# A unit of products with its low-weight matmuls set between the high-weight ones

## The chip, the core and the metric

The kernel runs on one core of one Trainium2 chip. The metric is the device time of one execution, in microseconds; "the time before" is the median of three runs of the kernel before.

## The reference

One layer of a streaming encoder for 512 frames of width 2048. The rows of `x` are normalised and multiplied by one wide matrix `w_in` (2048 x 12292): queries, keys, values and gates of three token mixers with four heads each, four forget-gate logits, and three merge gates of width 2048. The mixers are three kinds of attention (softmax with a forget bias, softmax over chunks with a relative bias, stick-breaking). Their outputs are gated, multiplied by `w_up`, weighted by the merge gates, summed, multiplied by `w_out` and added to `x`. All inputs and outputs are float32.

```python
hn = rmsnorm(x, norm_g)
proj = jnp.einsum('bsd,dc->bsc', hn, w_in)
br = proj[..., :QKVG_COLS].reshape(b, s, N_BRANCH, 4, BRANCH_W)
gates = jax.nn.sigmoid(proj[..., QKVG_COLS + N_HEADS:] + b_gate)
...                                    # ya, yb, yc: the three mixers
ys = jnp.stack([from_heads(ya), from_heads(yb), from_heads(yc)], axis=2)
ys = ys * jax.nn.silu(br[:, :, :, 3])
up = jnp.einsum('bsnw,nwd->bsnd', ys, w_up)
merged = jnp.sum(gates * up, axis=2)
return x + jnp.einsum('bsd,de->bse', merged, w_out)
```

## The kernel before

**Precision.** Every float32 operand is split into a high part (a rounded copy, written by ScalarE in `split`, L243) and a low part (the rest, by VectorE, L247). A product is the sum of three: high by high, high weights by low data, low weights by high data. In the names of the profile, `wh` and `wl` are the high and low weights; `x`, `t`, `m` and `y` are data that lie in `Parts`: 256 columns high, and beside them the same 256 columns low.

**Pairs, tasks and units.** The products with `w_in` and `w_out` are grouped by two blocks of 128 output columns (`PairTask`). A task replaces the eight products of a 2 x 2 block scheme (two column blocks, two halves of the frames, two halves of the inner width) by seven products of sums and differences, in the manner of Strassen. Each of the seven is a `Unit`: weights of eight tiles of 128 x 128, `UK = 8`, against eight data tiles of 256 frames. In a unit, the high weights of tile `j` meet high and low data in one matmul of 512 columns, which writes both halves of a PSUM bank; the low weights meet the high data in one of 256 columns, which adds to the left half. When the unit is done, ScalarE or VectorE takes the bank out (`after_of`), adding the two halves. A unit called `single` (the first task of the kernel, the first task with `w_out`, the last unit of all) uses only 256-column matmuls: two with high weights for each tile, one with low. The products with `w_up` (`up_units`) are plain ones with 512 columns throughout.

**The order.** The order of instructions on TensorE, ScalarE and VectorE is written out by a planner (`Flow`): each task is a generator that yields the engine, the cost and sometimes the due time of its next step, or an event that it waits for, and the planner picks the step that can start first. `mm_us` is the cost it takes for a matmul. The stream of units (`stream`, L1610) runs one unit after the other, with a slack so large that attention steps go first where they are ready; the weights are split two units ahead (`LA = 2`, three buffers for each of `wh` and `wl`). On TensorE the order is kept as planned: a matmul that waits holds up what stands behind it.

Within a unit (`mms_of`, L650) the order is: wait for `u.ready_hi` (ScalarE's split done; in `stream`), the eight products with high weights, wait for `u.ready` (VectorE's split done), the eight with low weights. All matmuls of this kind are issued by the helper `mm`, so they show as L262 in the profile.

Of the kernel before, what the change touches and what calls it, by code (L numbers as in the profile page):

```python
# [25 lines left out]
UK = 8  # L26
NQ = 4
HS = S // 2
# [7 lines left out]
PE, ACT, DVE = 0, 1, 2  # L36
# [112 lines left out]
def mm_us(n, x=1):  # L149
    return x * max(0.115, n / 2400 + 0.0133)  # L150
# [11 lines left out]
def hybrid_kernel(  # L162
# [16 lines left out]
    wp = ctx.enter_context(tc.tile_pool(name="wp", bufs=3))  # L179
    tp = ctx.enter_context(tc.tile_pool(name="tp", bufs=NT))  # L180
    sp = ctx.enter_context(tc.tile_pool(name="sp", bufs=8))
# [11 lines left out]
    spawn, set_, give = flow.spawn, flow.set, flow.give  # L193
    t2s, atts, raws, xps = Slots(NT, KEPT), Slots(4), Slots(NR), Slots(NX)
    accs = [Slots(2), Slots(1), Slots(1)]
# [7 lines left out]
    def acc(i=0):  # L203

        return pa.tile([P, S], F32, tag=f"acc{i}", name=nm("acc"), bufs=1 if i else 2)
# [10 lines left out]
    LH, RH = slice(0, HS), slice(HS, S)  # L216

    def two(ap):

        return ap.rearrange("p (h s) -> p h s", h=2)  # L220
# [40 lines left out]
    def mm(ps, w, x, start=False, stop=False, more=False):  # L261
        nc.tensor.matmul(ps, w, x, start=start, stop=stop, skip_group_check=more)  # L262
# [329 lines left out]
    class PairTask:  # L592
# [57 lines left out]
        def mms_of(self, i):  # L650
            p = self.order[i]
            bank = (0, 1, 2, 0, 0, 1, 2)[i] if self.late else {2: 1, 5: 2, 3: 2}.get(p, 0)
            onto = None if self.late else {6: 1, 7: 6, 4: 7, 3: 5}.get(p)
            more = onto is not None
            single = self.late or self.plain_end and p == 4
            self.bank = getattr(self, "bank", {})
            self.bank[p] = bank

            def go(u):
                if more:  # L660
                    yield self.ev[onto]
                    self.ps[p] = self.ps[onto]
                else:
                    yield accs[bank], 1
                    self.ps[p] = acc(bank)

                for j in range(UK):
                    yield lambda: self.ops[p](j) is not None
                    r, _, ev = self.ops[p](j)
                    yield ev  # L670
                    if single:
                        yield PE, mm_us(HS)
                        mm(self.ps[p][:, LH], u.hi[:, j, :], r[:, 0, :], j == 0 and not more, more=more)
                    else:
                        yield PE, mm_us(S)
                        mm(two(self.ps[p]), u.hi[:, j, :], r, j == 0 and not more, more=more)
                    if single:
                        yield PE, mm_us(HS)
                        mm(self.ps[p][:, LH], u.hi[:, j, :], r[:, 1, :], more=more)
                yield u.ready  # L680
                for j in range(UK):
                    yield PE, mm_us(HS)
                    mm(self.ps[p][:, LH], u.lo[:, j, :], self.ops[p](j)[1], stop=j == UK - 1, more=more)
            return go

        def after_of(self, i):
# [946 lines left out]


NT = 21
KEPT = 1
NX = 28
NR = 6
# [47 lines left out]
```

## Time and profile before

| | before |
|---|---|
| time, median of 3 runs | 1340.83 us (1339.83 to 1341.17) |
| span of the profiled execution, the only time that the profile gives for it | 1338.6 us |
| TensorE busy, matmuls | 1326.8 us (99%), 7546 |
| TensorE weight loads | 1158.2 us (87%), 7546 |
| VectorE busy | 1141.3 us (85%) |
| ScalarE busy | 806.2 us (60%) |
| granted TensorE clock | 1.000 |

The profile is of one execution. `PE` is TensorE's matmuls, `PEld` its weight loads, `DVE` VectorE, `ACT` ScalarE, `POOL` GpSimd, `SP` SyncE. A row of the timeline has start, length, engine, line, operation, output and inputs, the partitions and columns, and the count of like neighbours merged into it; a row of a group has a count, the busy time, the mean length of one in ns, and the idle time before it with what ended it. Matmuls are pipelined and their recorded ends are modelled, so neighbours overlap in the record: the pace is read from the starts.

### The profile page before, as it was taken

How to read it: one execution, taken by the hardware profiler on the slowest of the kernel's cores; microseconds unless marked ns; L12 is line 12 of the kernel's file. 1: busy time of each engine (PE TensorE's matmuls, PEld its weight loads, DVE VectorE, ACT ScalarE, POOL GpSimd, SP SyncE). 2: the span in 40 equal slices, each digit the busy share in tenths (PEclk: the TensorE clock that was granted, in tenths of full speed). 3: DMA queues.
4: the chain of work that ended last, by engine and by line, in shares of the span. 5: the costliest groups of instructions: out<-in, count | busy, mean ns of one | idle time of the engine just before them, and what ended most of it. 6: DMA issues, size and time to landing. Idle time of an engine off the chain costs nothing.

```text
span 1338.6 us, 20292 instructions
## 1 busy us (share of the span) xinstructions
PE 1326.8 (99%) x7546; PEld 1158.2 (87%) x7546; DVE 1141.3 (85%) x1691; ACT 806.2 (60%) x1274; POOL 97.9 (7%) x129
## 2 busy tenths in 40 slices
PE   8999999999999999999999999999999999999998
PEld 5888888888888888888888888888888888898887
DVE  7899888878888898888988879888888877797786
ACT  7766656556566655666567665566566645464443
POOL 0000000010100000000110100000010000000100
PEclk9999999999999999999999999999999999999999
DMA  9876677777776777777777677677777755659883
GB/s 307 231 194 163 174 190 201 184 187 181 185 218 163 209 200 182 210 175 197 201 189 190 171 203 189 183 186 189 187 182 250 281 197 177 202 152 258 239 243 103
DMA packets 92707, 265.23 MB, mean 198 GB/s; under 512 B 10528, under 2 KB 17312, under 8 KB 92608
## 3 DMA queue, kind: packets, MB, share of 16 engines
q1 hardware_dynamic: 72928, 202.77, 45.6%
q0 software_dynamic: 15552, 56.63, 25.6%
q10 hardware_dynamic: 4128, 4.53, 1.0%
q8 instruction: 59, 0.97, 0.3%
q14 instruction: 40, 0.33, 0.1%
HBM read 244.19 MB, written 19.70 MB: 197 GB/s over the span
## 4 chain that ended last, share of the span: by engine, by line
PE 96%; DVE 2%; DMA 1%; issue 0%; ACT 0%; DVEq 0%
PE acc L262 82%; PE att L262 8%; DMA raw<-in_w_col 1%; PE att L1124 1%; DVE wl L247 1%; PE att L1052 1%; PE att L257 1%; PE att L1200 1%; PE att L258 1%; PE att L1201 1%; PE att L259 1%; PE att L1199 1%; PE att L1151 0%; DVE m L247 0%; PE att L1302 0%
## 5 line engine op out<-in xcount | busy, mean ns | idle before, releaser
L247 DVE TENSOR_TENSOR wl<-raw,wh 128x1024 fp32r<-128x1024 f32 (+2 forms) x419 | 500.1, 1197 | 145.5 <-ACT wh L243 138.8
L243 ACT ACTIVATE wh<-raw 128x1024 fp32r<-128x1024 f32 (+2 forms) x419 | 434.6, 1039 | 135.6 <-PE acc L262 65.7
L262 PE MATMUL acc<-x,wh 128*128 128x512 f32 (+1 forms) x1568 | 400.5, 391 | 7.0 <-ACT wh L243 7.0
L262 PEld LDWEIGHTS acc<-x,wh 128*128 128x128 f32 x1568 | 277.3, 189 | 56.3 <-ACT wh L243 7.7
L262 PE MATMUL acc<-t,wh 128*128 128x512 f32 (+1 forms) x1128 | 282.2, 389 | 0.0
L262 PEld LDWEIGHTS acc<-t,wh 128*128 128x128 f32 x1128 | 198.5, 189 | 33.5
L262 PEld LDWEIGHTS acc<-x,wl 128*128 128x128 f32 x1504 | 207.0, 190 | 18.0 <-issue 1.7
L262 PE MATMUL acc<-x,wl 128*128 128x256 f32 (+1 forms) x1504 | 216.8, 285 | 0.6 <-DVE wl L247 0.6
L262 PEld LDWEIGHTS acc<-t,wl 128*128 128x128 f32 x1104 | 151.8, 190 | 11.4
L262 PE MATMUL acc<-t,wl 128*128 128x256 f32 x1104 | 156.2, 283 | 0.0
L282 POOL DMA_DIRECT2D raw<-in_w_col x92 | 79.7, 866 | 932.4 <-DMA raw<-in_w_col 469.0
L262 PE MATMUL acc<-m,wh 128*128 128x512 f32 (+1 forms) x512 | 114.1, 366 | 0.3 <-DVE m L247 0.2
L262 PEld LDWEIGHTS acc<-m,wh 128*128 128x128 f32 x512 | 85.4, 189 | 13.7 <-DVE m L247 1.1
L765 ACT ACTIVATE u<-acc 128x512 f32<-128x512 f32 x52 | 31.1, 599 | 75.3 <-PE acc L262 71.8
L819 ACT ACTIVATE c<-acc 128x256 f32<-128x256 f32 x51 | 19.6, 384 | 93.7 <-PE acc L262 90.6
L786 ACT ACTIVATE u<-acc 128x512 f32<-128x512 f32 x51 | 30.3, 594 | 72.7 <-PE acc L262 72.7
L635 DVE TENSOR_TENSOR raw<-raw,raw 128x1024 f32<-128x1024 f32 x54 | 65.8, 1219 | 0.4
L641 DVE TENSOR_TENSOR raw<-raw,raw 128x1024 f32<-128x1024 f32 x54 | 65.8, 1218 | 0.3
L262 PE MATMUL att<-y,wh 128*128 128x512 f32 x256 | 65.8, 389 | 0.0
L262 PEld LDWEIGHTS acc<-m,wl 128*128 128x128 f32 x448 | 60.5, 190 | 4.5 <-DVE wl L247 0.9
L262 PE MATMUL acc<-m,wl 128*128 128x256 f32 x448 | 62.6, 283 | 0.4 <-DVE wl L247 0.4
L769 ACT ACTIVATE v<-acc 128x512 f32<-128x512 f32 x52 | 31.2, 600 | 43.8 <-PE acc L262 43.3
(221 smaller groups left out, 1451.8 us busy)
## 6 DMA issues: line engine op xcount, KB each, us to landing
raw<-in_w_col SPq DMA_DIRECT2D x237, 512.0 KB, 4.5
raw<-in_w_col POOLq DMA_DIRECT2D x92, 512.0 KB, 6.8
raw<-in_w_out SPq DMA_DIRECT2D x40, 512.0 KB, 5.4
gl<-c SPq DMA_DIRECT2D x48, 256.0 KB, 4.1
raw<-in_w_up SPq DMA_DIRECT2D x32, 384.0 KB, 3.3
sg<-gl SPq DMA_DIRECT2D x48, 256.0 KB, 5.0
raw<-in_w_out POOLq DMA_DIRECT2D x16, 512.0 KB, 7.1
x<-in_xT SPq DMA_DIRECT2D x16, 256.0 KB, 7.3
```

Source lines behind the costliest of these rows:

```text
L243: nc.scalar.activation(hi, src, AF.Copy)
L247: nc.vector.tensor_sub(lo, src, f(hi))
L257: nc.tensor.matmul(ps, lh, rh, start=start, stop=False, skip_group_check=more)
L258: nc.tensor.matmul(ps, lh, rl, start=False, stop=False, skip_group_check=more)
L262: nc.tensor.matmul(ps, w, x, start=start, stop=stop, skip_group_check=more)
L282: nc.gpsimd.dma_start(to, src, accum_op=ALU.add)
L635: nc.vector.tensor_add(w[1], w[1], w[5])
L641: nc.vector.tensor_add(w[2], w[2], w[1])
L765: nc.scalar.activation(self.u, ps, AF.Copy)
L769: nc.scalar.activation(self.v, ps, AF.Copy)
L786: nc.scalar.activation(self.s, ps, AF.Copy)
L819: nc.scalar.activation(c, ps[:, RH], AF.Copy, scale=-1.0)
```

## The change

In a unit that isn't `single`, the 256-column matmul with the low weights of tile `j - 4` is put ahead of the 512-column matmul of tile `j`, for `j` from 4 to 7; the other four follow behind as before. Writing H for the 512-column matmuls and L for the 256-column ones, `HHHHHHHH LLLLLLLL` becomes `HHHH LHLHLHLH LLLL`. The wait for `u.ready` stands ahead of each L. The planner then writes out the whole order anew.

```diff
@@ mms_of
                     yield accs[bank], 1
                     self.ps[p] = acc(bank)
 
+                def low(j):
+                    yield u.ready
+                    yield PE, mm_us(HS)
+                    mm(self.ps[p][:, LH], u.lo[:, j, :], self.ops[p](j)[1], stop=j == UK - 1, more=more)
+
                 for j in range(UK):
+                    if j >= AHEAD and not single:
+                        yield from low(j - AHEAD)
                     yield lambda: self.ops[p](j) is not None
                     r, _, ev = self.ops[p](j)
                     yield ev
...
                     if single:
                         yield PE, mm_us(HS)
                         mm(self.ps[p][:, LH], u.hi[:, j, :], r[:, 1, :], more=more)
-                yield u.ready
-                for j in range(UK):
-                    yield PE, mm_us(HS)
-                    mm(self.ps[p][:, LH], u.lo[:, j, :], self.ops[p](j)[1], stop=j == UK - 1, more=more)
+                for j in range(0 if single else UK - AHEAD, UK):
+                    yield from low(j)
             return go
...
 NT = 21
+AHEAD = 4
 KEPT = 1
```

## The prediction

> **What bounds the kernel now.** I read the page first, then what TensorE waits for, then its order in time, then groups of matmuls in narrow stretches. Page: the span, TensorE's line, and the chain that ended last.
>
> ```profile
> span 1338.6 us, 20292 instructions
> PE 1326.8 (99%) x7546; PEld 1158.2 (87%) x7546; DVE 1141.3 (85%) x1691; ACT 806.2 (60%) x1274; POOL 97.9 (7%) x129
> PE 96%; DVE 2%; DMA 1%; issue 0%; ACT 0%; DVEq 0%
> ```
>
> TensorE is busy for 99% of the span and carries 96% of the chain. Its two largest waits (us in total, times, longest):
>
> ```profile
> PE acc L262 <- ACT wh L243: 7.0, 3, 6.6
> PE acc L262 <- DVE wl L247: 1.1, 2, 0.6
> ```
>
> They come to 8.1 us, 6.6 of it one wait. So the time changes only if the step from one matmul to the next changes, or if a new wait appears. The edit leaves the set of matmuls as it is; the question is what a step costs in another order. Timeline of TensorE (start, length, count): 256-column matmuls alone (61.70 to 63.62), 512-column ones alone (24 from 1118.52 to 1123.96), and two starts of the units that the edit changes, 43 units apart.
>
> ```profile
> 61.70 2.08 PE L262 MATMUL acc<-x,wh 128*128 128x256 f32 x16
> 63.62 1.12 PE L262 MATMUL acc<-x,wl 128*128 128x256 f32 x8
> ...
> 1118.52 1.98 PE L262 MATMUL acc<-y,wh 128*128 128x512 f32 x8
> ...
> 1123.96 0.39 PE L262 MATMUL att<-y,wh 128*128 128x512 f32 x1
> ...
> 1209.27 2.00 PE L262 MATMUL acc<-m,wh 128*128 128x512 f32 x8
> ...
> 1329.38 2.00 PE L262 MATMUL acc<-m,wh 128*128 128x512 f32 x8
> ```
>
> Alone, a 256 steps (63.62 - 61.70)/16 = 0.120 us and a 512 steps (1123.96 - 1118.52)/24 = 0.2267. A unit of eight and eight should take 8 x 0.2267 + 8 x 0.120 = 2.773 us; it takes (1329.38 - 1209.27)/43 = 2.793. **Each unit loses 20 ns**, with no wait in it. Groups in narrow stretches (count | busy, mean ns of one) show where: the 512s and the 256s of the unit that starts at 299.87, and 512s alone after 1118.
>
> ```profile
> L262 PE MATMUL acc<-x,wh 128*128 128x512 f32 x8 | 2.0, 392 | 0.0
> L262 PE MATMUL acc<-x,wl 128*128 128x256 f32 x8 | 1.1, 282 | 0.0
> L262 PE MATMUL att<-y,wh 128*128 128x512 f32 x9 | 2.5, 389 | 0.0
> ```
>
> Ends of matmuls are modelled: a record is some 162 ns longer than the step (389 against 227), so differences of records are differences of steps. The 512s behind a run of 256s lose 3 ns each, 24 a unit; nothing of the kind shows where sizes stay the same. The loss comes with the change of size.
>
> **The change part by part.** How many units: the low matmuls by form, over the whole span, are
>
> ```profile
> L262 PE MATMUL acc<-x,wl 128*128 128x256 f32 x1472 | 206.3, 282 | 0.6 <-DVE wl L247 0.6
> L262 PE MATMUL acc<-t,wl 128*128 128x256 f32 x1104 | 156.2, 283 | 0.0
> L262 PE MATMUL acc<-m,wl 128*128 128x256 f32 x448 | 62.6, 283 | 0.4 <-DVE wl L247 0.4
> ```
>
> 3024 in all, 378 units of eight, at 283 ns where settled. Two tasks of seven units and the last unit are "single" and stay as they are: 363 units change. In each, 8 high, 8 low becomes 4 high, then a low and a high by turns four times, then 4 low: five rises from 256 to 512 where there was one. The instruction order of the changed kernel shows this throughout; GpSimd and SyncE keep theirs entirely, VectorE and ScalarE but for a few neighbours near the end. No DMA moves, no instruction comes or goes. One nanosecond a unit is 0.363 us.
>
> *Price of a rise with short runs.* No stretch has single 256s between 512s; the nearest have two 512s (L948, L949) between low matmuls, and three 256s of attention (L257 to L259) between high ones:
>
> ```profile
> 204.31 0.86 PE L262 MATMUL acc<-t,wh 128*128 128x512 f32 x3
> ...
> 207.47 0.40 PE L262 MATMUL acc<-x,wh 128*128 128x512 f32 x1
> ...
> 371.41 0.87 PE L262 MATMUL acc<-t,wl 128*128 128x256 f32 x6
> ...
> 372.82 1.33 PE L262 MATMUL acc<-x,wh 128*128 128x512 f32 x5
> ...
> 376.10 0.63 PE L262 MATMUL acc<-t,wh 128*128 128x512 f32 x2
> ```
>
> From 204.31 to 207.47 stand eight 512s and eleven 256s: 3.16 us against 3.134 by the steps alone, 26 ns lost over two rises, 13 each. From 371.41 to 376.10 stand twelve 512s (ten from 372.82 on) and sixteen 256s: 4.69 against 4.640, 50 over two rises, 25 each. So a short run doesn't pass free; but a rise is paid over several 512s, not by the first alone. What one unsettled matmul costs (groups from 372.2 to 375.1, and from 375.4 on):
>
> ```profile
> L262 PE MATMUL acc<-x,wh 128*128 128x512 f32 x8 | 2.2, 396 | 0.0
> L262 PE MATMUL acc<-x,wl 128*128 128x256 f32 x8 | 1.1, 280 | 0.0
> ```
>
> An unsettled 512 loses 7 ns (396 against 389), an unsettled 256 gains 1 to 3 (282 or 280 against 283). In the changed unit no run is long enough to settle, so I take 7 for all eight 512s and -2 for all eight 256s: 56 - 16 = 40 ns a unit where 20 are lost now, **+20 ns, 363 times: +7.3 us**. Bounds: below, the loss vanishes (-20 ns, -7.3 us); above, each of the four added rises costs the full 20 of today's (+80 ns, +29 us). I take the value between because the 396 and 280 rows are the only ones whose surroundings stay unsettled for a whole unit.
>
> [...]
>
> *The low weights are wanted earlier*, by four 512s, 0.91 us, and a low matmul that waits now holds up the high ones queued behind it on TensorE. Three units: an ordinary one, and the two with the least room that I found (TensorE, then VectorE's split that it needs):
>
> ```profile
> 305.45 0.86 PE L262 MATMUL acc<-t,wh 128*128 128x512 f32 x3
> ...
> 685.49 1.12 PE L262 MATMUL acc<-x,wl 128*128 128x256 f32 x8
> ...
> 1205.43 1.21 PE L262 MATMUL acc<-m,wl 128*128 128x256 f32 x8 [0.45 <-DVE wl L247]
> ```
>
> ```profile
> 304.06 1.22 DVE L247 TENSOR_TENSOR wl<-raw,wh 128x1024 fp32r<-128x1024 f32 x1
> 683.35 1.22 DVE L247 TENSOR_TENSOR wl<-raw,wh 128x1024 fp32r<-128x1024 f32 x1
> 1204.16 2.35 DVE L247 TENSOR_TENSOR wl<-raw,wh 128x1024 fp32r<-128x1024 f32 x2
> ```
>
> At 1205.43 the split ends last already; four high matmuls that ran ahead of it now stand behind it: **+0.9 us**. At 685.49 the split ended at 684.57, 0.92 before: just in time. In the ordinary unit it ended at 305.28, and the lows, 0.91 after 305.45, come 1.1 later: free. The last high matmul also ends four lows, 0.48 us, later in its unit, and ScalarE's split for three units on waits for that buffer; the 1.1 cover it. Without that cover each late unit would pay up to 0.9. PSUM is read at the unit's end, which doesn't move.
>
> **Sum.** 7.3 + 0.9 = 8.2 us on the profiled execution, whose span of 1338.6 is 2.2 below the median of the runs, 1340.8; those 2.2 have no part in the change: 1340.8 + 8.2 = **1349.0**.
>
> **The rivals.**
> (a) *No change.* The loss belongs to a unit and not to a rise: 20 ns remain and only the wait is added, 1341.7. For: from 204.31 on two rises cost little more than one. Against: from 371.41 on they cost 50. [...] Chance 0.16.
> (b) *Faster: the run of lows is the cause.* A 256 leaves its successor's load only 120 ns; alone between 512s, each low has a long neighbour that makes up for it, and the 512s behind are at 389 again. Then the 20 ns go: -7.3 + 0.9, 1334.4. It decides if a single low is too short a run to unsettle what follows. Against: the 512s from 372.82 on are at 396 behind a run of only two. Chance 0.22; a further 0.04 that lows also step below 0.120, under 1333.
> (c) *The full price of a rise.* Each added rise costs 20 ns although one 512 follows: +29 + 0.9, 1371. Against: today 24 ns are spread over eight 512s. Chance 0.11.
> (d) *Waits.* The later splits of ScalarE push those of VectorE behind the lows; it decides where a lead falls under 0.91 us. Ten such units cost 9 us on top of (a): 1351. Against: the ordinary lead. Chance 0.03.
>
> **How the numbers follow.** The forecast has 0.44; its own range is 3 to 17 us more (a 512 at 5 to 9 ns, a 256 at -3 to -1), 1344 to 1358. About 0.2% is what a measurement of this kernel can tell from no change: 1338.1 to 1343.5. Faster: (b) with its tail, 0.26. Same: (a), 0.16. Slower: the forecast, (c) and (d), 0.58. The range takes in (b) and the forecast and leaves out (c) and the tail of (b), 0.15: 1333 to 1360.
>
> **What would show it.** Right: TensorE's timeline with units near 2.81 us; groups of 512s in them near 396 and of 256s near 281; a wait near 1205 on VectorE's split, 0.9 longer than now. Wrong: 512s at 389 in the changed units (b), 392 (a), above 400 (c), or waits on the split in many units (d).

## The result, and the profile after

The changed kernel takes 1346.6 us (median of four runs, 1345.2 to 1346.9) where the kernel before takes 1341.0 (1339.8 to 1341.2) beside it: 1.0043 times as long, 95% interval 1.003 to 1.0055. It is slower by 5.6 us. The prediction was 1349.0, range 1333 to 1360.

The page of the changed kernel, the lines that answer to those of before (span; busy time by engine; shares of the chain that ended last):

```profile
span 1345.0 us, 20293 instructions
PE 1331.6 (99%) x7546; PEld 1157.3 (86%) x7546; DVE 1142.9 (85%) x1691; ACT 807.0 (60%) x1274; POOL 97.6 (7%) x129
PE 93%; DVE 3%; DMA 2%; ACT 1%; issue 0%; DVEq 0%; ACTq 0%
```

The span is 6.4 us longer, TensorE is busy 4.8 longer with the same 7546 matmuls, and the other engines' busy times moved by under 2 us. So most of the time went into the pace of matmuls, and some into waits. TensorE's waits (us in total, times, longest):

```profile
PE acc L262 <- ACT wh L243: 7.7, 3, 6.6
PE acc L262 <- DVE wl L247: 2.0, 2, 1.4
```

They are 9.7 us where they were 8.1: 0.9 more on VectorE's split of low weights, 0.7 more on ScalarE's of high ones. The second lies near 59 us, in the kernel's first task, whose units are `single`; the first unit that the edit changes starts at 81 us. TensorE's timeline there, before and after:

```profile
58.72 2.18 PE L262 MATMUL acc<-x,wh 128*128 128x256 f32 x16 [0.23 <-ACT wh L243]
...
59.28 2.17 PE L262 MATMUL acc<-x,wh 128*128 128x256 f32 x16 [0.84 <-ACT wh L243]
```

ScalarE's split starts later there because its weights land later (57.23 us against 56.66, idle until a transfer from `w_in`). In the traces of the experiments this wait is anything from none (2, 3, 6, 7, 8) to 1.6 us (1), whatever the order of the units, so it is no part of what the edit does. The first is one place, and it is the edit's. TensorE's timeline there, and VectorE's split that ends the wait:

```profile
1207.43 1.12 PE L262 MATMUL acc<-m,wh 128*128 128x512 f32 x4
1208.72 2.35 DVE L247 TENSOR_TENSOR wl<-raw,wh 128x1024 fp32r<-128x1024 f32 x2
1209.99 0.39 PE L262 MATMUL acc<-m,wl 128*128 128x256 f32 x1 [1.44 <-DVE wl L247]
```

Four high matmuls run, then the first low one stands for 1.44 us in front of the other four: 0.99 more than the 0.45 of before. For the pace, an ordinary unit, with no wait and no attention step in it (TensorE's timeline: start, length):

```profile
301.28 1.09 PE L262 MATMUL acc<-x,wh 128*128 128x512 f32 x4
302.21 0.28 PE L262 MATMUL acc<-x,wl 128*128 128x256 f32 x1
302.32 0.40 PE L262 MATMUL acc<-x,wh 128*128 128x512 f32 x1
302.56 0.28 PE L262 MATMUL acc<-x,wl 128*128 128x256 f32 x1
...
303.61 0.65 PE L262 MATMUL acc<-x,wl 128*128 128x256 f32 x4
304.10 1.09 PE L262 MATMUL acc<-x,wh 128*128 128x512 f32 x4
```

From start to start it takes 304.10 - 301.28 = 2.82 us; the starts at full resolution give 2.813 in most such units, 40 ns over the 2.773 of the steps alone, where it was 20 over. And by groups over the whole span (count | busy, mean ns of one), two of before, then those of after:

```profile
L262 PE MATMUL acc<-x,wh 128*128 128x512 f32 x1504 | 392.0, 395 | 6.6 <-ACT wh L243 6.6
L262 PE MATMUL acc<-m,wh 128*128 128x512 f32 x384 | 96.3, 392 | 0.0
...
L262 PE MATMUL acc<-x,wh 128*128 128x512 f32 x1504 | 478.4, 398 | 6.6 <-ACT wh L243 6.6
...
L262 PE MATMUL acc<-x,wl 128*128 128x256 f32 x1472 | 322.9, 282 | 0.6 <-DVE wl L247 0.6
L262 PE MATMUL acc<-t,wl 128*128 128x256 f32 x1104 | 243.9, 282 | 0.0
L262 PE MATMUL acc<-m,wh 128*128 128x512 f32 x384 | 119.7, 396 | 0.0
```

The 512s stand at 396 to 398 where they stood at 392 to 395, the 256s at 282. Counted over all units from the starts of the matmuls in both traces: 273 units without an attention step lose 38.5 ns each on average where they lost 19.5, so 10.5 us where it was 5.3, **+5.2**. The 89 units with attention steps among their matmuls take 2 ns less each than they did, **-0.2**. The wait near 1205 us is **+1.0**. Together the edit costs +6.0; from the start of the first changed unit to the end the trace is 5.8 us longer (1263.4 against 1257.6), and the other 0.6 of the span's 6.4 is the later start.

### The profile page after: what moved, and what is told of

It is laid out like the page before. It is cut to its first block, busy times and chain, and to the rows that moved or that the text cites. A ratio compares the mean times of both kernels' runs of the same rounds, so it can differ in the third digit from the quotient of the medians.

```text
span 1345.0 us, 20293 instructions
## 1 busy us (share of the span) xinstructions
PE 1331.6 (99%) x7546; PEld 1157.3 (86%) x7546; DVE 1142.9 (85%) x1691; ACT 807.0 (60%) x1274; POOL 97.6 (7%) x129
## 4 chain that ended last, share of the span: by engine, by line
PE 93%; DVE 3%; DMA 2%; ACT 1%; issue 0%; DVEq 0%; ACTq 0%
PE acc L262 81%; PE att L262 6%; DMA raw<-in_w_col 2%; DVE wl L247 1%; PE att L1129 1%; DMA x<-in_xT 1%; PE att L1057 1%; PE att L257 1%; PE att L1206 1%; PE att L1205 1%; PE att L259 1%; PE att L258 1%; PE att L1204 1%; PE att L1156 0%; DVE m L247 0%
## 5 line engine op out<-in xcount | busy, mean ns | idle before, releaser
L262 PE MATMUL acc<-x,wh 128*128 128x512 f32 (+1 forms) x1568 | 486.9, 393 | 7.7 <-ACT wh L243 7.7
L262 PE MATMUL acc<-t,wh 128*128 128x512 f32 (+1 forms) x1128 | 347.0, 392 | 0.0
L262 PE MATMUL acc<-x,wl 128*128 128x256 f32 (+1 forms) x1504 | 333.5, 285 | 0.6 <-DVE wl L247 0.6
L262 PEld LDWEIGHTS acc<-x,wl 128*128 128x128 f32 x1504 | 257.2, 189 | 18.4 <-DVE wl L247 1.1
L262 PE MATMUL acc<-t,wl 128*128 128x256 f32 x1104 | 243.9, 282 | 0.0
L262 PEld LDWEIGHTS acc<-t,wl 128*128 128x128 f32 x1104 | 189.6, 189 | 11.7
L262 PE MATMUL acc<-m,wh 128*128 128x512 f32 (+1 forms) x512 | 137.6, 369 | 0.3 <-DVE m L247 0.2
L262 PE MATMUL acc<-m,wl 128*128 128x256 f32 x448 | 93.8, 282 | 1.4 <-DVE wl L247 1.4
L262 PEld LDWEIGHTS acc<-m,wl 128*128 128x128 f32 x448 | 74.0, 189 | 5.9 <-DVE wl L247 1.9
```

## The experiments

In all of them the loss of a unit is read from the starts of matmuls, in units without attention steps or waits: the period less 8 x 226.7 and 8 x 120 ns. This number says more than a single run's time: fifteen runs of the kernel before on one chip lay between 1339.2 and 1342.3 us. Experiments 1 to 4, 6 to 8 are one run each; the kernel before took 1341.08 beside the first four (one run) and 1340.17 (median) beside 5 to 8.

**1. All matmuls of one size.** The lows take all 512 columns, in the changed order.

```diff
-                    yield PE, mm_us(HS)
-                    mm(self.ps[p][:, LH], u.lo[:, j, :], self.ops[p](j)[1], stop=j == UK - 1, more=more)
+                    if single:
+                        yield PE, mm_us(HS)
+                        mm(self.ps[p][:, LH], u.lo[:, j, :], self.ops[p](j)[1], stop=j == UK - 1, more=more)
+                    else:
+                        yield PE, mm_us(S)
+                        mm(two(self.ps[p]), u.lo[:, j, :], self.ops[p](j)[0], stop=j == UK - 1, more=more)
```

> The changed order HHHH LHLHLHLH LLLL, but the matmuls with low weights take all 512 columns (high and low data), so that no size changes within a unit; the extra products (low by low) only make the result finer. Theory A (the loss comes with a rise from 256 to 512 columns): a unit takes 16 x 0.2267 = 3.627 us, loss 0, all records at 389 ns; in all 363 x 8 x 0.1067 = 310 us more for the added columns and 15 less for the loss of the changed kernel, about 1641 us. Rival B (the loss comes with the turns between high and low weights, whatever the size): the 512s stay near 396 and a unit loses some 40 ns, about 1656 us.

It took 1645.67 us, nearer to theory A's 1641 than to B's 1656. Groups of TensorE over the whole span:

```profile
L262 PE MATMUL acc<-m,wl 128*128 128x512 f32 x384 | 126.1, 389 | 0.0
L262 PE MATMUL acc<-m,wh 128*128 128x512 f32 x384 | 126.1, 389 | 0.0
```

Highs and lows, by turns or not, stand at the 389 of 512s alone in these units with `w_out` (groups with `w_in`, which hold the units with attention too, stand at 390 to 394), and the 244 undisturbed units lose 0, but for one. To alternate high and low weights cost nothing with all matmuls 512 wide; **the loss needs two sizes**.

**2 and 3. Fewer rises.** One low ahead (`HHHHHHH L H LLLLLLL`, two rises a unit), and the lows in twos (`HHHH LL HH LL HH LLLL`, three rises).

```diff
-AHEAD = 4
+AHEAD = 7
```

> Only one low matmul stands between the last two high ones: HHHHHHH L H LLLLLLL, two rises in a unit. Theory A with a price that is spread over the following 512s: the one 512 behind the single low pays part of it, a unit loses 25 to 30 ns. Theory A with a full price for each rise: 40 ns. Rival (the loss belongs to the unit and the change added only waits): 20 ns. No new wait, since the low is wanted only one 512 earlier: the wait near 1205 us stays at about 0.7.

```diff
-                    if j >= AHEAD and not single:
+                    if j >= AHEAD and not single and j % 2 == 0:
                         yield from low(j - AHEAD)
+                        yield from low(j - AHEAD + 1)
```

> The lows between the last four highs stand in twos: HHHH LL HH LL HH LLLL, three rises instead of five, the same four lows moved. If the loss counts rises (5 ns for each added one, as 20 for four in the changed kernel): 30 ns a unit. If it counts unsettled matmuls: 40 ns as in the changed kernel. If it belongs to the unit: 20.

With one ahead 1341.22 us, 26.7 ns a unit; in twos 1343.47, 33.3 ns. With 20 at one rise and 40 at five, the losses lie on a ladder of 6.7 ns. The second and the third rise cost 6.7 each; at that price the changed order with its five would lose 47, not 40, so a price for every rise does only roughly up to here. With one ahead TensorE waited 0.7 us near 1205, as expected:

```profile
PE acc L262 <- DVE wl L247: 1.2, 2, 0.7
```

**4. By turns from the start.** `AHEAD = 1` gives H L eight times, eight rises a unit. (The order written in the expectation, with two lows at the end, is a slip: there are none.)

> HLHLHLHLHLHLHLH LL (each low one tile behind its high): eight rises in a unit. If each added rise costs 5 ns: 20 + 7 x 5 = 55 ns a unit, 10 us on 273 undisturbed units. If the alternation settles into a pace of its own at 0.2267 + 0.120: 20 ns or less. If the loss is a fixed amount for an unsettled unit: 40. The low weights are wanted 1.6 us earlier than before, so there are more waits on the split: the one near 1205 us at about 2.0 us, and perhaps some others of under 1 us.

It took 1351.89 us, the slowest. But its units are of two kinds. TensorE's timeline, a stretch of 56 pairs of one high and one low, and one of 72 a little later:

```profile
693.60 0.39 PE L262 MATMUL acc<-t,wh 128*128 128x512 f32 x1
...
713.01 0.39 PE L262 MATMUL acc<-t,wh 128*128 128x512 f32 x1
...
719.54 0.40 PE L262 MATMUL acc<-t,wh 128*128 128x512 f32 x1
...
744.98 0.40 PE L262 MATMUL acc<-t,wh 128*128 128x512 f32 x1
```

(713.01 - 693.60)/56 = 346.6 ns a pair, exactly the 226.7 + 120 of the steps alone: no loss, with eight rises a unit. (744.98 - 719.54)/72 = 353.3: 53 ns a unit. Same instructions, no wait in either; the pace changes at the attention steps that lie between (some from 715.67 to 717.8) and then stays until the next ones. Of 268 undisturbed units 54 lose 2 ns or less, and 208 lose 57, 57 and 46 by turns. **No price for a rise can give both**, so the theory of the prediction, a price for each rise or for each unsettled matmul, falls here. What is left, as the author's reading, is a pace (346.6 or 353.3 ns a pair here) into which a row of equal periods locks, and which depends on how it was entered.

**5. Some units the other way round.** In three of seven products the lows come first, so that runs of equal size are twice as long and there are four rises in seven units.

```diff
+                first = p in (6, 7, 4) and not single
...
+                if first:
+                    yield from lows()
                 for j in range(UK):
...
+                if not first:
+                    yield from lows()
```

> The order of the kernel before, but in three of the seven units of a task (products 6, 7 and 4, which add onto a bank that is filled already) the eight lows stand first, so that they follow the lows of the unit before and their highs are followed by highs: four rises for seven units in place of seven, all runs long. Theory A (20 ns for a rise between long runs): 3 x 20 = 60 ns less for a task, some 50 tasks less those that attention disturbs, 2.2 to 3.0 us less than before: about 1338.4. Rival (20 ns belong to each unit): 1341. The lows of these units are wanted 1.8 us earlier: up to 1 us of new waits either way.

1341.33 us against 1340.17, ratio 1.0009 (1.0 to 1.0018). By time a miss: 1338.4 was expected. In the trace the loss is where the theory put it, 20 ns for each change from L to H (28 in the unit that holds it, less 7 in the one behind); over the undisturbed units that is 2.1 us less than before. But the lows at the head of a unit want VectorE's split eight matmuls earlier; TensorE's waits:

```profile
PE acc L262 <- ACT wh L243: 8.1, 4, 6.6
PE acc L262 <- DVE wl L247: 3.0, 2, 2.4
```

3.0 where it was 1.1, one of them 2.4 us: this ate what the pace gave. ScalarE's 1.1 more all lies ahead of the first unit whose order differs (0.9 of it near 60 us), in the start that varies from execution to execution. The two terms cancel, so the 1.2 us by which the median is higher aren't accounted for; its interval reaches down to no change.

**6. Pairs throughout.** From here on the order of a unit is a word of sixteen letters:

```diff
+                h, l = iter(range(UK)), iter(range(UK))
+                for c in "HHHHHHHHLLLLLLLL" if single else order_of(self, i):
+                    yield from high(next(h)) if c == "H" else low(next(l))
```

Here it is `HHLL` four times.

> HHLL four times in every unit: four rises, runs of two, a period that never ends. The run with strict alternation showed two paces for the same order, 346.7 and 353.7 ns for a high and a low. If such an order locks as well: a unit loses 0 in some stretches and a multiple of 6.7 ns for each period in others (27 for one such step a period), constant from one attention step to the next. If the loss counts unsettled matmuls: 40 ns everywhere.

1339.31 us. TensorE's timeline, the second pair of a unit and the last unit, 163 blocks of `HHLL` later:

```profile
1217.64 0.63 PE L262 MATMUL acc<-m,wh 128*128 128x512 f32 x2
1218.11 0.39 PE L262 MATMUL acc<-m,wl 128*128 128x256 f32 x2
...
1331.19 2.07 PE L262 MATMUL acc<-m,wh 128*128 128x256 f32 x16
```

(1331.19 - 1217.64)/163 = 696.6 ns a block against 693.3 by the steps: 3.3 lost, 13.3 a unit, and the same 13 or 14 in 261 of 272 undisturbed units, whatever stood before. That is neither branch of the expectation: one pace and not two, and a third of the 40. Four rises lose 13.3 here; the kernel before loses 20 with one, the changed kernel 40 with five. The count of rises alone doesn't tell the loss.

**7. The changed order for `w_in` alone.** Products with `w_out` keep the order of before.

```diff
+    def order_of(task, i):
+        return "HHHHLHLHLHLHLLLL" if task.rest is None else "HHHHHHHHLLLLLLLL"
```

> The changed order in the products with w_in alone; those with w_out keep the order of before. Theory (20 ns more for each undisturbed unit, and a wait near 1205 us that the four lows make longer): the wait is 0.5 us again, the 48 units of w_out take 2.793 us instead of 2.813, so 1.0 + 1.0 us less than the changed kernel, about 1344.6.

1343.60 us, 3.0 less than the changed kernel. TensorE's waits, and one group:

```profile
PE acc L262 <- ACT wh L243: 7.1, 2, 6.9
PE acc L262 <- DVE wl L247: 1.1, 2, 0.6
```

```profile
L262 PE MATMUL acc<-m,wh 128*128 128x512 f32 x384 | 96.2, 392 | 0.0
```

The wait near 1205 is back at 0.5 us, and the 48 units with `w_out` lose 20 again: 0.9 + 48 x 0.020 = 1.9 us. From the start of the first changed unit to the end this trace is 1.8 us shorter than that of the changed kernel (1261.7 against 1263.4); the rest of the 3.0 is its start, where ScalarE's wait near 59 us is missing.

**8. Fourteen ways in.** After a unit of eight and eight, one unit of some other word, and behind it H L by turns.

```diff
+    def order_of(task, i):
+        if i in (0, 3):
+            return "HHHHHHHHLLLLLLLL"
+        if i in (1, 4):
+            seen.append(0)
+            return entries[(len(seen) - 1) % len(entries)]
+        return "HL" * 8
```

> In every task the units 1 and 4 stand in the order of before, the units behind them enter strict alternation (HLHL...) by one of fourteen ways, and the units behind those alternate. If the pace of the alternation is decided by how it is entered, each way gives the same pace, 346.7 or 353.7 ns for a pair, wherever nothing else stands between: some ways give loss-free units (0 ns), others 53 to 57. If it is decided by something else (which data, which place in the kernel), the same way gives both.

1345.27 us. Loss in ns of the unit with the word, and of the pure H L unit behind it, some of the fourteen:

```
HHLLHLHLHLHLHLHL    4 to 5     then 0
HHHHLLLLHLHLHLHL   17 to 20    then 0
HHHHLHLHLHLHLLLL   12 to 15    then 5 to 6, then 0 or 1
HHHLLHLHLHLHLHLL   36          then 47
HHHHHLLLLLHLHLHL   38 to 39    then 58
HLHLHLHLHLHLHLHL   58 to 59    then 46
```

Each row stands on two to four undisturbed places, and the same word gave the same pace in each. **The way in decides.** The third word is the order of the changed kernel: behind eight and eight it loses 12 to 15; behind itself, as in the changed kernel, 40.

**9 and 10. Entered with care, and pairs.** Experiment 9 enters H L by the first of these words, anew after each attention step (`flow.others` counts them); 10 is experiment 6. In both the first `w_out` task whose sizes change keeps the order of before, so that the wait near 1205 doesn't grow.

```diff
+    def order_of(task, i):
+        if task.rest is not None and len(waited) < 7:
+            waited.append(0)
+            return "HHHHHHHHLLLLLLLL"
+        if flow.others != at_last[0]:
+            at_last[:] = flow.others, 0
+        at_last[1] += 1
+        return {1: "HHHHHHHHLLLLLLLL", 2: "HHLLHLHLHLHLHLHL"}.get(at_last[1], "HL" * 8)
```

> Strict alternation HLHL... entered by the way that left 0 to 5 ns of loss behind it (a unit HHHHHHHH LLLLLLLL, then HHLLHLHLHLHLHLHL), anew after each attention step; the first task with w_out that changes size keeps the order of before, so that no split comes later than its low. If the entry decides the pace: some 200 alternating units at 0 to 1 ns, 38 entering ones at 4, 49 at 20; the 273 undisturbed units lose about 1.2 us in place of 5.3, with at most 0.5 us of new waits: 3.5 to 4.2 us less than before, about 1336.5. If strict alternation falls back into its slow pace behind some of the entries: up to 57 ns for each such unit, 1341 or more.

> HHLL throughout, except in the first task with w_out that changes size, which keeps the order of before. A unit lost 13.3 ns wherever it was undisturbed; 273 units x 6.7 ns = 1.8 us less than before; the wait near 1205 us back at 0.5 instead of 1.8. So 1.5 to 2 us less than before, about 1338.4, a little under the limit of what can be told.

Experiment 9: 1338.03 us against 1340.24, 0.9985 (0.9976 to 0.9994). Experiment 10: 1338.89, 0.9986 (0.9977 to 0.9995), 1.4 us less where 1.5 to 2 were expected. Both intervals lie below 1, by little; 9 stayed 1.5 us above what it should. In its trace the units with `w_in` lose 0 or 1 as meant, but with `w_out` no attention step comes any more, so the counter never begins anew, and all 41 units there start straight with H L behind eight and eight, the bad way in: 57, 57, 46.

**11. Two matmuls swapped.** The counter is set to 1 in that first `w_out` task.

```diff
         if task.rest is not None and len(waited) < 7:
             waited.append(0)
+            at_last[1] = 1
```

The one unit behind it begins `HHLL` and not `HLHL`: two neighbouring matmuls change places, and nothing else does.

> Differs from the kernel e9_entered in two neighbouring matmuls out of 7529: the first alternating unit of the products with w_out starts HHLLHL... and not HLHLHL.... There the 41 units behind it lose 57, 57 and 47 ns by turns in e9. If the entry alone decides the pace: all 41 lose 0 to 1 ns, the first 4, and the stretch from there to the end is 41 x 53.6 ns = 2.2 us shorter, about 1335.8 and 0.3% less than before. If the pace belongs to these units (their data, their place): 57 as before, 1338.0.

1336.46 us against 1340.24, 0.9968 (0.9957 to 0.998), on another chip than experiment 9. TensorE's timeline of experiment 9, from that place to the last unit (`mm` has moved to L264 in these two kernels):

```profile
1215.12 0.40 PE L264 MATMUL acc<-m,wh 128*128 128x512 f32 x1
1215.35 0.28 PE L264 MATMUL acc<-m,wl 128*128 128x256 f32 x1
...
1331.01 2.08 PE L264 MATMUL acc<-m,wh 128*128 128x256 f32 x16
```

And of experiment 11:

```profile
1215.31 0.63 PE L264 MATMUL acc<-m,wh 128*128 128x512 f32 x2
1215.78 0.39 PE L264 MATMUL acc<-m,wl 128*128 128x256 f32 x2
1216.00 0.40 PE L264 MATMUL acc<-m,wh 128*128 128x512 f32 x1
...
1329.02 2.07 PE L264 MATMUL acc<-m,wh 128*128 128x256 f32 x16
```

41 units take 115.89 us in the one and 113.71 in the other: 2.827 and 2.773 each, a loss of 53 ns and of none, over the whole rest of the kernel, with one swap at its head. The chain that ended last has it in one step (start, length, matmuls), in experiment 9

```profile
1202.89 131.18 PE acc L264 x752
```

and in experiment 11

```profile
1203.08 128.98 PE acc L264 x752
```

with the same number of matmuls in it. Of all versions this is the fastest, 3.8 us below the kernel before.

## Why the prediction was right, and where its steps were off

**Direction and size.** Slower was forecast with 0.58, at +8.2 us; measured +5.6 (spans +6.4, of which 0.6 is the start). No transfer, and no engine but VectorE at one wait, had a part in it, as the prediction said. (It said too that VectorE and ScalarE keep their order but for neighbours near the end; two pairs of neighbours on ScalarE in the middle of the kernel change places as well, and nothing hangs on that.)

**The loss of a unit.** Forecast 40 ns where 20 are lost; measured 40 where 20 are lost, in four of five undisturbed units (means 38.5 and 19.5), with groups at 396 to 398 and 282 where 396 and 281 were named. The number was right, but not for the reason given, that no run is long enough to settle: `HHLL` has no run over two and loses 13, H L by turns none over one and loses 0 or 53. That the number fitted this order was luck. The prediction's own rows spoke against the reason: its 512s at 396 stand in a run of ten, longer than the runs of eight at 392. The lower end of the forecast's own range, 3 us more, doesn't follow from its terms either: 512s at 5 and 256s at -3 lose 16 ns a unit, 4 less than before, and with the wait that is 0.6 us less.

**The count, the term that was mis-sized.** "+20 ns, 363 times" took each unit as undisturbed. 89 have attention steps among their matmuls, and these became 2 ns shorter each, not 20 longer. So the pace cost 5.2 - 0.2 = +5.0 where the prediction had +7.3. The rows for it were there, in part: the two stretches around L257 and L948 lost 26 and 50 ns over eleven and sixteen small matmuls, more than the 20 of a clean unit. They were read as the price of a rise, and not as the state of every unit that holds attention.

**The wait near 1205.** Forecast +0.9 on VectorE's split; measured 0.99 there. ScalarE's splits were put at nothing, and rightly: the 0.7 more that TensorE waited for them lies near 59 us, ahead of the first changed unit. So the edit cost 5.0 + 1.0 = 6.0 us where 8.2 were forecast, and nearly all of the difference is in the count.

**The rivals.** (a) a loss for each unit, indifferent to order: no, by the 40 ns. (c) the full price of each rise: no. (d) waits in many units: no, one place. (b) single lows that step at full pace between highs: not in this change, but it exists. Experiments 4, 8, 9 and 11 show hundreds of pairs at 346.6 ns. (The 120 ns that (b) gives to a load can be read in the trace of before: the first weight load of the unit at 299.87 us starts at 299.75, with the 256 ahead. That the loss comes from loads is not shown.) The prediction asked whether a single low is too short to unsettle what follows; the runs say that this is decided by the way in, and the changed order, entered by itself, loses 40 in most of its units.

**What the order is worth.** Experiments 9 and 11 hold the same matmuls with the same loads, and they differ by 2.2 us without a wait (131.18 and 128.98 us for the 752 matmuls of the chain's last step). So rival (a)'s indifference to the order falls by these runs too. No order went below 346.6 ns a pair in the long run, the 226.7 + 120 that the sizes take alone.

**What stays open.** That two sizes are needed (experiment 1) and that for H L by turns the way in decides (8 and 11) is shown. Experiment 1 widens the lows and with that gives them other data and both halves of the bank; it doesn't part the one from the other. What keeps a pace once it is entered, and why the losses lie 6.7 ns apart, is not shown. The records of the weight loads don't tell it: near 1270 us they start 2 to 5 ns behind the start of a matmul in experiment 9 and in 11 alike.

## What to carry to other kernels

When an engine is busy for 99% and an edit only reorders its instructions, price the edit by the period of a whole undisturbed unit, and count only the units that are undisturbed; a sum of prices for single neighbours can be right once and wrong for the next order. Where matmuls of two sizes with a new weight each must be mixed, either take an order whose loss doesn't depend on what came before (two and two lost 13 or 14 ns in nearly every undisturbed unit) or fix how the row is entered (H L by turns lost 0 or 53 ns a unit by the entry alone in experiments 11 and 9), and look at the trace for where it is disturbed. An operand that was wanted earlier turned its producer's late end into a longer stall of all that stood behind (1.44 us where it was 0.45): look for the one unit with the least room, it was 1 of the 6 us here. And before a longer wait is put down to an edit, look where it stands: the other wait that had grown lay ahead of all that was changed.

## What the runs showed of the hardware that was not expected

Sixteen matmuls, eight of 512 and eight of 256 columns with a new weight tile each, took 2.773 us plus 0 to 59 ns (in experiment 5 also 7 ns less, in the unit behind a change from L to H), by their order and by what ran before. In a row of like units the losses seen are near 0, 13, 20, 27, 33 and 40, and 57, 57, 46 by turns. Such a pace held for over 100 us (41 units, 115.89 and 113.71 us, in experiments 9 and 11) and was seen to change where something else came between (in experiment 4 from 346.6 to 353.3 ns a pair, at the attention steps from 715.67 to 717.8 us). The 57, 57, 46 is a period of three pairs: in experiment 9 the steps near 1270 us are 233, 117, 241, 120, 236 and 113 ns, over and over, 1060 for three pairs where experiment 11 takes 1040. With sixteen of 512 columns the loss was 0 in 243 of 244 undisturbed units (experiment 1).
